# Diffusion backbone with a Conformer and an mLSTM layer: the seam before the last MLP and the last output rows rearranged

## The chip, the cores and the metric

The kernel runs on one core of one Trainium2 chip. The metric is the device time of one execution in microseconds (us), as the median of several runs; lower is better.

## The reference, cut to what matters

Two layers work on 256 latent tokens (the stream that is returned) and 256 context tokens of width 1024. What the change touches is the end of the second layer, on the latent tokens alone:

```python
h = layer_norm(ALPHA * h + g1 * y, ln1_g[i], ln1_b[i])            # y: the mLSTM's output, through w_down
h = layer_norm(ALPHA * h + g2 * sq_relu_mlp(modulate(h, sh2, sc2), mlp_w1[i], mlp_w2[i]), ln2_g[i], ln2_b[i])
# sq_relu_mlp(u) = square(relu(u @ w1)) @ w2        w1: 1024x4096, w2: 4096x1024
# sh1, sc1, g1, sh2, sc2, g2 = split(silu(c) @ ada_w[i] + ada_b[i], 6)      "adaLN", each 1024 wide
```

The gate `g2` comes from the last two of twelve blocks of 512 columns ("units" 10 and 11) of `ada_w[1]`; it is wanted only when the MLP's result is added.

## The kernel before, in words

Every matrix product is done in single precision by splitting both operands into a high and a low part (`split`: ScalarE rounds the high part, L152, VectorE subtracts for the low part, L153) and adding three products in PSUM. The weights stream in 1 MB loads through three buffers named `raw` on SyncE's queue and are split into `wh`/`wl` (or `wx`, a separate set of eight).

The rows of the stream lie in `R` (in the trace `res`): 128 partitions, two blocks t = 0, 1 of 128 tokens, 1024 columns, used as two halves (`HF`). The names below are those of the trace: `mm` (three PSUM banks), `ln`, `cv` (two each), `fl` (one) are PSUM tiles, `E`, `S`, `L` small scratch tiles of 512 columns, `mv` mean, variance and 1/sqrt of a row, `G` the gate rows.

**The seam.** `down` accumulates the mLSTM's output product in four banks `acc[t][hf]`. `residual` (L1632, L1633, L1636) multiplies a bank by the gate row, adds it to `R` and takes row statistics, all on VectorE. `row_norm` aggregates them (L1641), ScalarE takes the root (L1642), VectorE the reciprocal (L1645); `ln1_rows` scales the rows (L1651). TensorE transposes the scaled rows (`turn`, L1683, into `ln` and, for one half, `cv`), and `ln1` applies gain and modulation and writes the MLP's input `x` in high and low part: for three of the four tiles ScalarE writes the high part and a full copy in `S` (L1697) and VectorE subtracts (L1698), for the fourth VectorE does it all (L1694). Between the transposes of t = 0 and t = 1 stands one adaLN unit (`ada_unit`, L335: eight small matmuls of 32 columns each, into the bank `fl`). Unit 11 follows only after the first quarter of the MLP's first product, just before the second product; its 1 MB loads share the `raw` buffers with the weights.

**The MLP** runs in four parts c. In each, `gemm` makes eight blocks of hidden values (L190, L191; the first four of c = 0 together, in three `mm` banks and one `cv`), `e1` squares them (L200, L201, L1763), and `w2_mm` adds their product (L206 to L208) to the four banks `acc[t][hf]` (two `ln`, two `cv`), which stay open over all four parts.

**The end.** In c = 3 the last six blocks are held back (`last`), and each of the four banks is finished in turn with 18 matmuls of 512 columns. After each, `residual` runs on VectorE. When both halves of t = 0 are in, `finish(0)` normalises: ScalarE scales (L1745), GpSimd multiplies by the gain row (L1746) and adds the bias row (L1747), each half is stored. `finish(1)` does the same on VectorE (L1751, L1754); the two last stores end the kernel.

The order of instructions on each engine is set when the program is built, from the code and from a planner's times; each engine then runs its list in order and waits on semaphores. `tc.issue_after(x)` places what follows behind x, `tc.keep_in_program_order` pins an instruction, `pin` does so for the adaLN matmuls.

Of the kernel before, what the change touches and what calls it, by code (L numbers as in the profile page):

```python
# [8 lines left out]
F32 = mybir.dt.float32  # L9
# [5 lines left out]
P = 128  # L15
# [55 lines left out]
def hybrid_kernel(ctx: ExitStack, tc: tile.TileContext, xT, vecs_d, wdw_d, ada0_w, ada_w, wg_d, pw1a, pw1, pw2, w1_0, w2_0,  # L71
# [28 lines left out]
    def psum(tag="mm"):  # L100
        return pp.tile([P, 512], F32, tag=tag, name=nm(tag), bufs={"mm": 3, "ln": 2, "fl": 1, "cv": 2}[tag])
# [43 lines left out]

    def raw_load(src):
        raw = wp.tile([P, 2048], F32, tag="raw", name=nm("raw"), bufs=3)
        nc.sync.dma_start(raw[:, :src.shape[-1]], src)
        return raw

    def split(hi, lo, src):
        c = nc.scalar.copy(hi, src)  # L152
# [1485 lines left out]
    def row_norm(t, pinned=False):  # L1638

        st_, mv = nst[t]  # L1640
        nc.vector.bn_aggr(mv[:, 0:2], st_.rearrange("p h c -> p (h c)"))  # L1641
        o = nc.scalar.activation(mv[:, 2:3], mv[:, 1:2], AF.Sqrt, bias=eps)  # L1642
        if pinned:
            tc.keep_in_program_order(o)
        nc.vector.reciprocal(mv[:, 2:3], mv[:, 2:3])  # L1645
        return mv

    def ln1_rows(t, pinned=False):
        mv = row_norm(t, pinned)
        for g_ in range(2):  # L1650
            o = nc.vector.tensor_scalar(R[:, t, HF[g_]], R[:, t, HF[g_]], mv[:, 0:1], mv[:, 2:3], op0=ALU.subtract,  # L1651
                                        op1=ALU.mult)
        return o.ins
# [25 lines left out]
    def turn(t, g_, tag="ln"):  # L1679

        tr = psum(tag)
        for i in range(4):
            nc.tensor.transpose(tr[:, i * P:(i + 1) * P], R[:, t, g_ * 512 + i * P:g_ * 512 + (i + 1) * P], ident)  # L1683
        return tr

    def ln1(tr, t, g_, vector=False):

        ts = BLK[t]
        y = tmp("SL"[vector])
        for i in range(4):  # L1690
            f, sl = 4 * g_ + i, slice(i * P, (i + 1) * P)
            for o_ in (u2[f][:, ts], y[:, sl]):
                if vector:
                    nc.vector.tensor_scalar(o_, tr[:, sl], ca[:, 1, f:f + 1], cb[:, 1, f:f + 1],  # L1694
                                            op0=ALU.mult, op1=ALU.add)
                else:
                    nc.scalar.activation(o_, tr[:, sl], AF.Identity, scale=ca[:, 1, f:f + 1], bias=cb[:, 1, f:f + 1])  # L1697
            nc.vector.tensor_tensor(u2[f][:, C + t * P:C + (t + 1) * P], y[:, sl], u2[f].bitcast(F32)[:, ts],  # L1698
                                    op=ALU.subtract)
# [38 lines left out]

    def finish(t):
        mv = row_norm(t)  # L1740
        o_ = [tmp("E") for _ in range(2)]
        if t == 0:
            nc.vector.scalar_tensor_tensor(mv[:, 3:4], mv[:, 0:1], -1.0, mv[:, 2:3], op0=ALU.mult, op1=ALU.mult)
            for hf in range(2):
                nc.scalar.activation(o_[hf], R[:, t, HF[hf]], AF.Identity, scale=mv[:, 2:3], bias=mv[:, 3:4])  # L1745
                nc.gpsimd.tensor_tensor(o_[hf], o_[hf], GN[:, HF[hf]], op=ALU.mult)  # L1746
                nc.gpsimd.tensor_tensor(o_[hf], o_[hf], BN[:, HF[hf]], op=ALU.add)  # L1747
                nc.sync.dma_start(out[t * P:(t + 1) * P, HF[hf]], o_[hf])
        else:
            for hf in range(2):  # L1750
                nc.vector.scalar_tensor_tensor(o_[hf], R[:, t, HF[hf]], mv[:, 0:1], GN[:, HF[hf]],  # L1751
                                               op0=ALU.subtract, op1=ALU.mult)
            for hf in range(2):
                nc.vector.scalar_tensor_tensor(o_[hf], o_[hf], mv[:, 2:3], BN[:, HF[hf]], op0=ALU.mult, op1=ALU.add)  # L1754
                nc.sync.dma_start(out[t * P:(t + 1) * P, HF[hf]], o_[hf])

    acc = None
    for c in range(4):
        hid = {}

        def e1(m, ps):
            r_, q_ = joined(ps), tmp("E")[:, :C]
            nc.vector.scalar_tensor_tensor(q_, r_, 0.0, r_, op0=ALU.max, op1=ALU.mult)  # L1763
            t_ = HD(F32R)
            hid[m] = t_[:, :C], t_[:, C:]
            split(*hid[m], q_)

        gemm(w1_1, range(4 * c, 4 * c + 4), u2, T, e1, ko=0 if c else 3 + Z.pre4, pre=pre1 if c == 0 else None)
        if c == 0:
            ada_unit()  # L1770
            acc = [[psum("ln") for _ in range(2)], [psum("cv") for _ in range(2)]]
            for i, t_ in enumerate(G5):
                rows(t_, rows_d[i + 1:i + 2])
        elif c < 3:
            if c == 1:
                gate2()
            rescale(c - 1)

        def w2_mm(w, kt, t, hf):
            ts = BLK[t]  # L1780
            mm3t(acc[t][hf], hid[kt][0][:, ts], hid[kt][1][:, ts], w[0][hf], w[1][hf],
                 c == 0 and kt == 0, c == 3 and kt == DT - 1)

        last = []
        for k2 in range(4):
            raw = raw_load(w2_1[4 * c + k2])
            for i in range(2):
                kt = 2 * k2 + i
                if c == 3 and k2 == 1:
                    last.append((kt, split_w(raw[:, i * 1024:(i + 1) * 1024], WX)))  # L1790
                    continue
                w = split_w(raw[:, i * 1024:(i + 1) * 1024])
                w = [[w_[:, sl] for sl in HF] for w_ in w]
                if c == 3 and k2 > 1:
                    last.append((kt, w))
                else:
                    for t in range(2):
                        for hf in range(2):
                            w2_mm(w, kt, t, hf)
        if last:  # L1800
            nc.scalar.activation(con.tile([P, 1], F32, name=nm("warm")), eps, AF.Sqrt)
            for t in range(2):
                for hf in range(2):
# [83 lines left out]
```

## Time and profile before

| | before |
|---|---|
| median of 3 runs | 1698.73 us |
| lowest, highest | 1697.41, 1699.22 us |
| the profiled execution: its own time | 1699.18 us |
| the profiled execution: span of the core | 1697.5 us |
| TensorE busy in the span | 98% |
| VectorE, ScalarE, GpSimd busy | 61%, 44%, 3% |

The span runs from the first to the last event of the core in the trace; the execution's own time lies 1.7 us above it. Rows of a timeline give the start in us from the span's beginning, the duration in us, the engine (PE is TensorE's matmuls, PEld its weight loads, DVE VectorE, ACT ScalarE, POOL GpSimd, SP SyncE with its DMA queue), the code line, the operation, output and inputs, a count, and in brackets the idle time just before with what ended it. A matmul's end is modelled, and neighbours overlap: the step from one start to the next tells what it costs.

### The profile page before, as it was taken

To read this page: it belongs to the slowest core of one execution; us is meant where nothing else is said; L and a number is where in the kernel's file an instruction comes from. 1 tells how busy PE (TensorE), PEld (TensorE's weight loads), DVE (VectorE), ACT (ScalarE), POOL (GpSimd) and SP (SyncE) were. 2 spreads that over 40 slices of the span, in tenths; PEclk is the share of its full clock that TensorE was granted. 3 is DMA by queue.
4 is the path that set the end of the run, shared out by engine and by line. 5 is a ranking of instruction groups with operands and counts; after the bars stand their busy time and mean duration, and the time that the engine had idled before them with its cause. 6 is when DMAs were issued, how large, how long until landed. Compare 5 with 4: busy or idle time off the path is not lost.

```text
span 1697.5 us, 22796 instructions
## 1 busy us (share of the span) xinstructions
PE 1669.2 (98%) x8878; PEld 1363.8 (80%) x8878; DVE 1033.0 (61%) x1841; ACT 744.0 (44%) x1195; POOL 44.3 (3%) x92
## 2 busy tenths in 40 slices
PE   7999999999999999999999999999999999999997
PEld 5655898878888998876788899888877878878886
DVE  5555795666645776751243653563487786776676
ACT  3312563232324476642333533442477564645443
POOL 0000000000000000000000000000011120000001
PEclk9999999999999999999999999999999999999999
DMA  8546322434424065567765752454454556756552
GB/s 340 198 156 243 111 75 95 157 128 146 145 100 148 2 211 180 183 238 252 251 214 174 251 181 105 155 189 171 157 190 176 193 195 209 257 211 229 192 184 89
DMA packets 70828, 300.54 MB, mean 177 GB/s; under 512 B 7170, under 2 KB 22018, under 8 KB 40384
## 3 DMA queue, kind: packets, MB, share of 16 engines
q1 hardware_dynamic: 53056, 284.39, 47.6%
q10 hardware_dynamic: 17664, 14.69, 2.7%
q8 instruction: 70, 1.15, 0.3%
q14 instruction: 38, 0.31, 0.1%
HBM read 283.32 MB, written 15.73 MB: 176 GB/s over the span
## 4 chain that ended last, share of the span: by engine, by line
PE 92%; DVE 5%; ACT 1%; issue 1%; DMA 1%; POOL 0%; SPq 0%; DVEq 0%; POOLq 0%; ACTq 0%
PE mm L175 17%; PE mm L178 17%; PE mm L179 17%; PE mm L190 7%; PE mm L191 4%; PE mm L206 3%; PE mm L207 3%; PE mm L208 3%; PE cv L208 2%; PE cv L207 2%; PE cv L206 2%; PE fl L335 1%; DVE wl L153 1%; PE fl L748 1%; PE cv L830 1%
## 5 line engine op out<-in xcount | busy, mean ns | idle before, releaser
L153 DVE TENSOR_TENSOR wl<-raw,wh 128x1024 fp32r<-128x1024 f32 x346 | 424.7, 1233 | 275.8 <-ACT wh L152 271.4
L152 ACT CAST wh<-raw 128x1024 fp32r<-128x1024 f32 x346 | 360.6, 1050 | 494.5 <-PE mm L178 269.0
L178 PE MATMUL mm<-u,wh 128*128 128x512 f32 (+1 forms) x808 | 292.9, 363 | 0.1
L175 PE MATMUL mm<-u,wh 128*128 128x512 f32 (+1 forms) x680 | 245.5, 361 | 0.2 <-ACT E L770 0.2
L179 PE MATMUL mm<-u,wl 128*128 128x512 f32 (+1 forms) x680 | 242.3, 357 | 0.0
L178 PEld LDWEIGHTS mm<-u,wh 128*128 128x128 f32 x808 | 153.4, 190 | 23.5 <-issue 1.8
L175 PEld LDWEIGHTS mm<-u,wh 128*128 128x128 f32 x680 | 129.2, 190 | 28.8 <-issue 9.1
L179 PEld LDWEIGHTS mm<-u,wl 128*128 128x128 f32 x680 | 129.2, 190 | 18.4 <-issue 0.2
L175 PE MATMUL mm<-xm,wh 128*128 128x512 f32 x256 | 102.2, 399 | 0.0
L206 PE MATMUL mm<-wh,xl 128*128 128x512 f32 x256 | 101.3, 396 | 0.5 <-ACT wh L152 0.5
L207 PE MATMUL mm<-wh,xl 128*128 128x512 f32 x256 | 100.9, 394 | 0.0
L179 PE MATMUL mm<-xm,wl 128*128 128x512 f32 x256 | 99.9, 390 | 0.0
L208 PE MATMUL mm<-wl,xl 128*128 128x512 f32 x256 | 99.6, 392 | 0.0
L175 PE MATMUL mm<-hid,wh 128*128 128x512 f32 (+1 forms) x256 | 93.1, 364 | 0.0
L178 PE MATMUL mm<-hid,wh 128*128 128x512 f32 (+1 forms) x256 | 92.8, 363 | 0.0
L179 PE MATMUL mm<-hid,wl 128*128 128x512 f32 (+1 forms) x256 | 92.7, 362 | 0.0
L190 PE MATMUL mm<-x,wh 128*128 128x512 f32 x232 | 81.0, 398 | 0.8 <-DVE x L1698 0.8
L416 DVE SCALAR_TENSOR_TENSOR S<-ar,cs,S 128x512 f32<-128x512 f32 x56 | 40.8, 749 | 61.3 <-DMA ar<-ada_w 61.0
L178 PE MATMUL mm<-qq,wh 128*128 128x272 f32 x256 | 73.9, 289 | 0.0
L175 PE MATMUL mm<-qq,wh 128*128 128x272 f32 x256 | 73.5, 289 | 0.0
L179 PE MATMUL mm<-qq,wl 128*128 128x272 f32 x256 | 73.5, 288 | 0.0
L190 PE MATMUL mm<-u,wh 128*128 128x512 f32 x192 | 68.6, 399 | 0.0
(507 smaller groups left out, 3277.8 us busy)
## 6 DMA issues: line engine op xcount, KB each, us to landing
raw<-w SPq DMA_DIRECT2D x64, 1024.0 KB, 4.8
raw<-wo SPq DMA_DIRECT2D x32, 1024.0 KB, 4.9
raw<-ada_w SPq DMA_DIRECT2D x26, 1024.0 KB, 5.9
ar<-ada_w SPq DMA_DIRECT2D x80, 256.0 KB, 3.4
raw<-wv SPq DMA_DIRECT2D x16, 1024.0 KB, 5.4
raw<-wqT SPq DMA_DIRECT2D x16, 1024.0 KB, 5.6
raw<-wq SPq DMA_DIRECT2D x16, 1024.0 KB, 4.9
raw<-wk SPq DMA_DIRECT2D x16, 1024.0 KB, 5.2
```

The lines of the kernel that those rows point to most:

```text
L152: c = nc.scalar.copy(hi, src)
L153: nc.vector.tensor_tensor(lo, src, hi.bitcast(F32), op=ALU.subtract)
L175: a = nc.tensor.matmul(ps, wh, xh, start=start, stop=False)
L178: nc.tensor.matmul(ps, wh, xl, start=False, stop=False)
L179: lastmm[0] = nc.tensor.matmul(ps, wl, xh, start=False, stop=stop).ins
L190: todo = [lambda s_, e_: nc.tensor.matmul(ps, wh, r[0], start=s_, stop=e_), lambda s_, e_: nc.tensor.matmul(ps[:, :n], wl, r[0][:, :n], st ...
L191: lambda s_, e_: nc.tensor.matmul(ps[:, :n], wl, r[0][:, :n], start=s_, stop=e_)]
L206: nc.tensor.matmul(ps, xh, wh, start=start, stop=False)
L207: nc.tensor.matmul(ps, xl, wh, start=False, stop=False)
L208: nc.tensor.matmul(ps, xh, wl, start=False, stop=stop)
L335: a = nc.tensor.matmul(ps[32 * j:32 * j + 32], cs[:, kt, 14 - 2 * v:46 - 2 * v], blocks[kt], start=first and kt < 4, stop=last and kt >= 4 ...
L416: nc.vector.scalar_tensor_tensor(a, w, c, a, op0=ALU.mult, op1=ALU.add)
```

## The change

It has three parts.

At the seam the banks `fl` and one `mm` change places, so that `fl` holds `acc[0][1]` instead of `acc[1][1]`. The rows of t = 0 are scaled by ScalarE (with a small VectorE operation for the offset) instead of VectorE. The four subtractions for the low parts of the first tile (`lows`) come behind the scaling of t = 1. Both adaLN units are loaded ahead of the seam, unit 11 as eight loads of 256 KB into tiles `pw` that the mLSTM has left; its first half stands behind unit 10, its second half behind the transposes of t = 1. The place before the MLP's second product is gone.

At the end `acc[1][1]` is closed after the first two blocks and added to `R` early (`part`). The remaining six blocks of that half are computed as two quarters of 256 columns in two fresh `mm` banks, each with its own residual and statistics (`quarter`).

Of the output rows t = 0, GpSimd does the first half and the lower 256 columns of the second; the upper 256 go to VectorE (`rest`), behind the statistics of the third quarter. `finish(1)` writes to `S` tiles.

```diff
     def raw_load(src):
-        nc.sync.dma_start(raw[:, :src.shape[-1]], src)
+        loaded[0] = nc.sync.dma_start(raw[:, :src.shape[-1]], src).ins
...
-                acc.extend([[psum(), psum()], [psum(), psum("fl")]])
+                acc.extend([[psum(), psum("fl")], [psum(), psum()]])
...
     def ln1_rows(t, pinned=False):
         mv = row_norm(t, pinned)
+        if t == 0:
+            o = nc.vector.scalar_tensor_tensor(mv[:, 3:4], mv[:, 0:1], -1.0, mv[:, 2:3], op0=ALU.mult, op1=ALU.mult)
+            for g_ in range(2):
+                nc.scalar.activation(R[:, t, HF[g_]], R[:, t, HF[g_]], AF.Identity, scale=mv[:, 2:3], bias=mv[:, 3:4])
+            return o.ins
...
-    def ada_unit():
+    def ada_unit(blocks, kts=range(DT)):
         pin[0] = True
-        ada_n3.mm()
+        ada_n3.mm(blocks, kts)
         pin[0] = False
 
-    ln1(turn(0, 0), 0, 0)
+    units = [ada_load(1, 10)]
+    with tc.issue_after(loaded[0]):
+        units.append(ada_load(1, 11, PW))
+    y0 = ln1(turn(0, 0), 0, 0, low=False)
     tr1 = turn(0, 1, "cv")
 
     scaled = ln1_rows(1, True)
-    ada_unit()
+    ada_unit(units[0])
+    ada_unit(units[1], range(4))
     with tc.issue_after(scaled):
+        lows(y0, 0, 0)
         ln1(turn(1, 0), 1, 0)
         tr2 = turn(1, 1)
+        ada_unit(units[1], range(4, 8))
         ln1(tr1, 0, 1, True)
         ln1(tr2, 1, 1)
...
-                nc.gpsimd.tensor_tensor(o_[hf], o_[hf], GN[:, HF[hf]], op=ALU.mult)
-                nc.gpsimd.tensor_tensor(o_[hf], o_[hf], BN[:, HF[hf]], op=ALU.add)
-                nc.sync.dma_start(out[t * P:(t + 1) * P, HF[hf]], o_[hf])
...
+            for o, sl in ((o_[0], HF[0]), (o_[1][:, LO], slice(512, 768))):
+                nc.gpsimd.tensor_tensor(o, o, GN[:, sl], op=ALU.mult)
+                nc.gpsimd.tensor_tensor(o, o, BN[:, sl], op=ALU.add)
+            nc.sync.dma_start(out[0:P, HF[0]], o_[0])
+            return o_[1]
...
+    def part(ps, sl):
+        e_ = tmp("E")[:, :ps.shape[-1]]
+        nc.vector.tensor_tensor(e_, ps, G2[:, sl], op=ALU.mult)
+        return nc.vector.tensor_tensor(R[:, 1, sl], R[:, 1, sl], e_, op=ALU.add)
+
+    def quarter(q, ps=None):
+        sl = slice(q * C, (q + 1) * C)
+        if ps is not None:
+            part(ps, sl)
...
+        return nc.vector.bn_stats(nst[1][0][:, q, :], R[:, 1, sl]).ins
+
+    def rest(o, behind):
+        sl = slice(768, 1024)
+        with tc.issue_after(behind):
+            nc.vector.tensor_tensor(o[:, HI], o[:, HI], GN[:, sl], op=ALU.mult)
+            nc.vector.tensor_tensor(o[:, HI], o[:, HI], BN[:, sl], op=ALU.add)
+        nc.sync.dma_start(out[0:P, HF[1]], o)
...
         if c == 0:
-            ada_unit()
...
-                 c == 0 and kt == 0, c == 3 and kt == DT - 1)
+                 c == 0 and kt == 0, c == 3 and kt == (1 if t and hf else DT - 1))
...
-            for t in range(2):
-                for hf in range(2):
-                    for kt, w in last:
-                        w2_mm(w, kt, t, hf)
-                    residual(t, hf, acc[t][hf], G2)
-                finish(t)
+            for hf in range(2):
+                for kt, w in last:
+                    w2_mm(w, kt, 0, hf)
+                residual(0, hf, acc[0][hf], G2)
+                if hf == 0:
+                    part(acc[1][1], HF[1])
+            held = finish(0)
+            for kt, w in last:
+                w2_mm(w, kt, 1, 0)
+            part(acc[1][0], HF[0])
+            for q in range(2):
+                quarter(q)
+            for q, sl in HALVES:
+                ps = psum()[:, :C]
+                for i, (kt, w) in enumerate(last):
+                    mm3t(ps, hid[kt][0][:, BLK[1]], hid[kt][1][:, BLK[1]], w[0][1][:, sl], w[1][1][:, sl],
+                         i == 0, i == len(last) - 1)
+                behind = quarter(2 + q, ps)
+                if q == 0:
+                    rest(held, behind)
+            finish(1)
```

How the instructions stand. The line numbers of the changed kernel are its own: L1690 is the transpose (before L1683), L337 the adaLN matmul (L335), L1710 ScalarE's copies (L1697), L1644 the root (L1642).

TensorE at the seam, before, from the transposes of t = 0 to those of t = 1 (`raw` holds an adaLN unit):

```order
L1683 MATMUL ln_13057<-ident,res 128x128 x4
L1683 MATMUL cv_13075<-ident,res 128x128 x4
L335 MATMUL fl_13085<-raw_13086,cs 32x512 x4
L335 MATMUL fl_13085<-raw_13088,cs 32x512 x4
L1683 MATMUL ln_13098<-ident,res 128x128 x4
L1683 MATMUL ln_13116<-ident,res 128x128 x4
```

The same place now, behind the transposes of t = 0 (`raw` is unit 10, `pw` unit 11):

```order
L337 MATMUL fl_13102<-raw_13058,cs 32x512 x4
L337 MATMUL fl_13102<-raw_13060,cs 32x512 x4
L337 MATMUL fl_13102<-pw_13062,cs 32x512
L337 MATMUL fl_13102<-pw_13064,cs 32x512
L337 MATMUL fl_13102<-pw_13066,cs 32x512
L337 MATMUL fl_13102<-pw_13068,cs 32x512
L1690 MATMUL ln_13119<-ident,res 128x128 x4
L1690 MATMUL ln_13137<-ident,res 128x128 x4
L337 MATMUL fl_13102<-pw_13070,cs 32x512
L337 MATMUL fl_13102<-pw_13072,cs 32x512
L337 MATMUL fl_13102<-pw_13074,cs 32x512
L337 MATMUL fl_13102<-pw_13076,cs 32x512
```

Unit 11's eight matmuls have come from behind the first quarter of the MLP to both sides of the transposes of t = 1.

ScalarE at the same place, before: the last of the eight copies of t = 0, the root of t = 1, and what follows:

```order
L1697 ACTIVATE x_13052<-ln_13057,cb_13045,ca_13044 128x128
L1697 ACTIVATE S_13062<-ln_13057,cb_13045,ca_13044 128x128
L1642 ACTIVATE mv_13006<-mv_13006,eps 128x1
L152 CAST wx_13158<-raw_13156 128x512
L1697 ACTIVATE x_13049<-ln_13098,cb_13045,ca_13044 128x128
```

And now:

```order
L1710 ACTIVATE x_13053<-ln_13078,cb_13046,ca_13045 128x128
L1710 ACTIVATE S_13083<-ln_13078,cb_13046,ca_13045 128x128
L1644 ACTIVATE mv_13007<-mv_13007,eps 128x1
L1710 ACTIVATE x_13050<-ln_13119,cb_13046,ca_13045 128x128
L1710 ACTIVATE S_13124<-ln_13119,cb_13046,ca_13045 128x128
```

The root stands behind the same eight copies; the weight cast behind it has moved to a later place.

VectorE at the end, before, from the multiply of the third bank on:

```order
L1632 TENSOR_TENSOR E_14701<-cv_13400,row_13151 128x512
L1633 TENSOR_TENSOR res<-res,E_14701 128x512
L1636 BN_STATS st_14704<-res 128x6
L1632 TENSOR_TENSOR E_14725<-cv_13401,row_13151 128x512
L1633 TENSOR_TENSOR res<-res,E_14725 128x512
L1636 BN_STATS st_14704<-res 128x6
L1641 BN_AGGR mv_14705<-st_14704 128x2
```

And now (`E_14689` is the held second half of the output rows t = 0):

```order
L1781 TENSOR_TENSOR E_14716<-cv_13413,row_13178 128x512
L1782 TENSOR_TENSOR res<-res,E_14716 128x512
L1790 BN_STATS st_14719<-res 128x6 x2
L1781 TENSOR_TENSOR E_14742<-mm_14723,row_13178 128x256
L1782 TENSOR_TENSOR res<-res,E_14742 128x256
L1790 BN_STATS st_14719<-res 128x6
L1795 TENSOR_TENSOR E_14689<-E_14689,row_13181 128x256
L1796 TENSOR_TENSOR E_14689<-E_14689,row_13182 128x256
L1781 TENSOR_TENSOR E_14768<-mm_14749,row_13178 128x256
L1782 TENSOR_TENSOR res<-res,E_14768 128x256
L1790 BN_STATS st_14719<-res 128x6
L1643 BN_AGGR mv_14720<-st_14719 128x2
```

Behind the last bank stand three operations of 256 columns instead of three of 512, and ahead of them two that GpSimd did.

More of the change, by code (lines that the diff above doesn't have):

```diff
@@ L147, in raw_load @@
         raw = wp.tile([P, 2048], F32, tag="raw", name=nm("raw"), bufs=3)
-        nc.sync.dma_start(raw[:, :src.shape[-1]], src)
+        loaded[0] = nc.sync.dma_start(raw[:, :src.shape[-1]], src).ins
         return raw
+    loaded = [None]
     def split(hi, lo, src):
@@ L1684, in turn, with lows, ln1 @@
         return tr
-    def ln1(tr, t, g_, vector=False):
+    def lows(y, t, g_):
+        for i in range(4):
+            f = 4 * g_ + i
+            nc.vector.tensor_tensor(u2[f][:, C + t * P:C + (t + 1) * P], y[:, i * P:(i + 1) * P],
+                                    u2[f].bitcast(F32)[:, BLK[t]], op=ALU.subtract)
+    def ln1(tr, t, g_, vector=False, low=True):
         ts = BLK[t]
@@ L1740, in finish @@
         mv = row_norm(t)
-        o_ = [tmp("E") for _ in range(2)]
+        o_ = [tmp("ES"[t]) for _ in range(2)]
         if t == 0:
@@ L1745, in finish @@
                 nc.scalar.activation(o_[hf], R[:, t, HF[hf]], AF.Identity, scale=mv[:, 2:3], bias=mv[:, 3:4])
-                nc.gpsimd.tensor_tensor(o_[hf], o_[hf], GN[:, HF[hf]], op=ALU.mult)
-                nc.gpsimd.tensor_tensor(o_[hf], o_[hf], BN[:, HF[hf]], op=ALU.add)
-                nc.sync.dma_start(out[t * P:(t + 1) * P, HF[hf]], o_[hf])
-        else:
-            for hf in range(2):
[L1751 to L1755, printed above, removed]
+            for o, sl in ((o_[0], HF[0]), (o_[1][:, LO], slice(512, 768))):
[4 more added lines that the diff above has]
+        for hf in range(2):
+            nc.vector.scalar_tensor_tensor(o_[hf], R[:, t, HF[hf]], mv[:, 0:1], GN[:, HF[hf]],
+                                           op0=ALU.subtract, op1=ALU.mult)
+        for hf in range(2):
+            nc.vector.scalar_tensor_tensor(o_[hf], o_[hf], mv[:, 2:3], BN[:, HF[hf]], op0=ALU.mult, op1=ALU.add)
+            nc.sync.dma_start(out[t * P:(t + 1) * P, HF[hf]], o_[hf])
+    def part(ps, sl):
[7 more added lines that the diff above has]
+        if q == 0:
+            nst[1] = con.tile([P, 4, 6], F32, name=nm("st")), con.tile([P, 4], F32, name=nm("mv"))
+        return nc.vector.bn_stats(nst[1][0][:, q, :], R[:, 1, sl]).ins
[5 more added lines that the diff above has]
+        nc.sync.dma_start(out[0:P, HF[1]], o)
     acc = None
@@ L1801, in hybrid_kernel @@
             nc.scalar.activation(con.tile([P, 1], F32, name=nm("warm")), eps, AF.Sqrt)
-            for t in range(2):
-                for hf in range(2):
-                    for kt, w in last:
-                        w2_mm(w, kt, t, hf)
-                    residual(t, hf, acc[t][hf], G2)
-                finish(t)
+            for hf in range(2):
+                for kt, w in last:
[15 more added lines that the diff above has]
+                behind = quarter(2 + q, ps)
+                if q == 0:
+                    rest(held, behind)
+            finish(1)
     close_pool()
```

6 lines of the change are left out of this document (4 added, 2 removed).

## The prediction

> **What bounds the kernel now.** I read the page first, then the waits of the seam, then the timelines of the seam and of the end, engine by engine. The page says what the kernel lives on:
>
> ```profile
> PE 1669.2 (98%) x8878; PEld 1363.8 (80%) x8878; DVE 1033.0 (61%) x1841; ACT 744.0 (44%) x1195; POOL 44.3 (3%) x92
> ```
>
> TensorE is busy for 98% of the span, so time comes only from TensorE work taken out of its list, from its few gaps, or from the stretch behind its last matmul. The waits between 1486 and 1516 us (engine, line, whom it waited for, us in total, times, longest) hold three of those gaps; the two stretches below them (us, then busy time of PE, PEld, DVE, ACT, POOL, then clock, DMA share and GB/s) show TensorE busy for 2.22 of 4 us behind 1504 and the DMA queues empty before 1500:
>
> ```profile
> PE ln L1683 <- DVE res L1651: 1.3, 1, 1.3
> PE mm L190 <- DVE x L1698: 0.8, 1, 0.8
> PE fl L335 <- DVE E L1632: 0.5, 1, 0.5
> ...
> 1496.00:1500.00 4.00, 4.00 (x20) 3.30 (x19) 3.50 (x8) 0.29 (x1) 0.00 (x0) 1.00 0.00 0
> ...
> 1504.00:1508.00 4.00, 2.22 (x14) 1.84 (x15) 3.70 (x14) 2.92 (x9) 0.00 (x0) 1.00 0.90 334
> ```
>
> At the other end the chain that ended last (start, us, engine, tile, line) leaves TensorE with its last matmul and is VectorE's alone; the timeline row under it is the aggregation, from which on the change leaves every operation as it is:
>
> ```profile
> 1688.43 0.70 DVE E L1632
> 1689.15 1.39 DVE res L1633
> 1690.57 0.70 DVE st L1636
> ...
> 1691.29 0.21 DVE L1641 BATCH_NORM_AGGREGATE mv<-st 128x2 f32<-128x12 f32 x1
> ```
>
> From the last matmul to the aggregation pass 2.86 us (1688.43 to 1691.29). So the change can earn at three places: adaLN unit 11, the gaps of the seam, these 2.86 us.
>
> **Unit 11 leaves its old place.** TensorE's timeline there:
>
> ```profile
> 1529.37 0.39 PE L190 MATMUL mm<-x,wh 128*128 128x512 f32 x1
> 1529.69 1.92 PE L335 MATMUL fl<-raw,cs 128*32 128x512 f32 x16
> 1531.55 0.50 PE L206 MATMUL ln<-wh,hid 128*128 128x512 f32 x1
> ```
>
> From the L190 matmul to the first of the second product pass 2.18 us. With the unit gone the step is that of a 512-column matmul, and the rows of 18 of them in a bank of the end give it:
>
> ```profile
> 1680.07 0.39 PE L206 MATMUL cv<-wx,hid 128*128 128x512 f32 x1
> ...
> 1684.15 0.39 PE L206 MATMUL cv<-wx,hid 128*128 128x512 f32 x1
> ```
>
> 4.08 us for 18 is 0.23 each, so the place gives back 2.18 - 0.23 = 1.95 us, fully on the path, since nothing else ends there. It is earned only if the eight matmuls fit into the gaps of the seam; a unit costs TensorE 1.86 us there (1529.69 to 1531.55), a half 0.93.
>
> **The seam.** Its rows, by engine:
>
> ```profile
> 1501.77 1.92 PE L335 MATMUL fl<-raw,cs 128*32 128x512 f32 x16 [0.51 <-DVE E L1632]
> 1505.01 1.09 PE L1683 MATMUL ln<-ident,res 128*128 128x128 f32 x8 [1.32 <-DVE res L1651]
> 1506.86 0.50 PE L190 MATMUL mm<-x,wh 128*128 128x512 f32 x1 [0.77 <-DVE x L1698]
> ...
> 1498.07 1.00 DVE L1651 TENSOR_SCALAR res<-res,mv 128x512 f32<-128x512 f32 x2
> 1498.99 0.68 DVE L1632 TENSOR_TENSOR E<-mm,G 128x512 f32<-128x512 f32 x1
> 1504.32 1.00 DVE L1651 TENSOR_SCALAR res<-res,mv 128x512 f32<-128x512 f32 x2
> 1506.52 0.29 DVE L1698 TENSOR_TENSOR x<-S,x 128x128 fp32r<-128x128 f32 x1 [0.24 <-ACT S L1697]
> ...
> 1502.93 0.48 ACT L1697 ACTIVATE x<-ln,cb,ca 128x128 fp32r<-128x128 f32 x1
> 1503.28 0.49 ACT L1697 ACTIVATE S<-ln,cb,ca 128x128 f32<-128x128 f32 x1
> 1503.79 0.29 ACT L1642 ACTIVATE mv<-mv,eps 128x1 f32<-128x1 f32 x1
> ```
>
> *The bank.* TensorE was free at 1501.26 and stood 0.51 us for `fl`, which VectorE still had to read. With `fl` as `acc[0][1]` it is read two banks sooner, and the gap goes: the units start at 1501.26.
>
> *Rows of t = 0 on ScalarE.* The end of the kernel has the same pair of operations:
>
> ```profile
> 1683.21 0.16 DVE L1743 SCALAR_TENSOR_TENSOR mv<-mv 128x1 f32<-128x1 f32 x1
> 1683.47 1.52 ACT L1745 ACTIVATE E<-res,mv 128x512 f32<-128x512 f32 x2 [0.48 <-DVE mv L1743]
> ...
> 1500.00 0.59 PEld L1683 LDWEIGHTS ln<-ident,res 128*128 128x128 f32 x4
> ```
>
> ScalarE begins 0.26 us behind the small operation's start and needs 1.52 for both halves: 1498.07 + 0.26 + 1.52 = 1499.85, just ahead of the transposes' first weight load at 1500.00, which TensorE reaches no sooner. It costs nothing, with 0.15 us to spare for the first half and more for the second. VectorE is free some 0.7 us sooner (about 1498.25 instead of 1498.99), and its two interposed subtractions go behind the scaling. But the root of t = 1 still follows ScalarE's eight copies: the last starts at 1503.28, they step by 0.35, so the root starts at 1503.63 instead of 1503.79. All that VectorE wins shrinks to 0.16 us. The scaling then starts at 1504.16, the transposes at 1504.85, and the first complete `x`, which came at 1506.81 with its subtraction, at 1506.65; VectorE has the four postponed subtractions done by then (2 x 0.5 for the scaling, 4 x 0.2: 1505.96).
>
> *TensorE's list.* Unit 10 from 1501.26 to 1503.12, half of unit 11 to 1504.05: hidden, as the transposes wait until 1504.85. They take 1.09 to 1505.94, the second half 0.93 to 1506.87. Before, the first product began at 1506.86, so by these rows it starts as before; if the transposes' busy time holds some overlap it starts at 1506.70. I take 0.1 us of gain, with 0 and 0.16 as ends. If the cover of the second half were gone it would cost 0.93. The copy of `fl` to scratch now stands in VectorE's list behind the second low part and waits for the second half; behind it are the low parts of the third `x` and on, which TensorE wants only after eight pairs of matmuls of 512 and 256 columns, 8 x (0.23 + 0.12) = 2.8 us (the 0.12 is shown below). It costs nothing.
>
> *The loads.* Unit 11 is moved ahead of a weight load on SyncE's queue. The queue's rows, and the landing times of the quarter size:
>
> ```profile
> 1480.91 6.87 SPq L148 DMA_DIRECT2D raw<-ada_w  x2
> 1491.71 0.33 SPq L148 DMA_DIRECT2D raw<-w  x1
> ...
> ar<-ada_w SPq DMA_DIRECT2D x80, 256.0 KB, 3.4
> ```
>
> The second load of unit 10 is out by 1487.8. The eight behind it, at 0.33 us each, are out by about 1490.5 if none waits for an earlier landing; the weight load behind them waited for its buffer until 1491.71 anyway. All 2 MB have until 1503 to 1506 to land, and from 1496 to 1500 the queues carried nothing. I cost it at nothing. The later weight loads come sooner, as two loads have left their ring of buffers; the planner now casts two more of them ahead of the hidden values' copies, which delays those by two casts. The only sign of that resource in the trace is a wait of 0.2 us:
>
> ```profile
> PEld mm L190 <- DVE E L201: 0.2, 1, 0.2
> ```
>
> Each later block of hidden values is again 2.8 us of matmuls, which pass before its bank is wanted, so I take 0, with 0.3 as a loss.
>
> Seam: 1.95 + 0.1 = 2.05 us, between 1.65 and 2.1.
>
> **The end.** First TensorE: two consecutive matmuls of 256 columns step by 0.12 us,
>
> ```profile
> 589.73 0.28 PE L175 MATMUL mm<-hid,wh 128*128 128x256 f32 x1
> 589.85 0.28 PE L178 MATMUL mm<-hid,wh 128*128 128x256 f32 x1
> ```
>
> so two quarters take 36 x 0.12 = 4.32 us instead of 4.08, and TensorE ends 0.24 us later. The early `part` runs beside the first banks, in VectorE's waits. Then GpSimd against VectorE:
>
> ```profile
> 1685.07 1.18 DVE L1633 TENSOR_TENSOR res<-res,E 128x512 f32<-128x512 f32 x1
> ...
> 1684.41 1.29 POOL L1746 TENSOR_TENSOR E<-E,row 128x512 f32<-128x512 f32 x1 [284.53 <-PE cv L208]
> 1685.78 1.62 POOL L1747 TENSOR_TENSOR E<-E,row 128x512 f32<-128x512 f32 x1
> 1687.36 1.28 POOL L1746 TENSOR_TENSOR E<-E,row 128x512 f32<-128x512 f32 x1
> 1688.72 1.26 POOL L1747 TENSOR_TENSOR E<-E,row 128x512 f32<-128x512 f32 x1
> ...
> L201 DVE TENSOR_TENSOR E<-mm,E 128x256 f32<-128x256 f32 x47 | 19.8, 421 | 14.9 <-ACT E L200 14.8
> ```
>
> VectorE's add of two SBUF operands, some 0.7 us by itself, took 1.18 and 1.39 where GpSimd was at work, and both ended 0.55 us behind the end of a GpSimd operation (1685.70 to 1686.25; 1689.98 to 1690.53), while the multiply of a PSUM bank at 1688.43 kept its 0.70. The Trainium skill's page "SBUF — State Buffer", section "Who interferes with whom", says that a VectorE instruction with two SBUF inputs and a GpSimd instruction that reads SBUF lock each other out for a whole instruction, whichever starts first; these rows agree. By that rule `rest`, itself two such operations, meets GpSimd too.
>
> Now the walk. Up to the end of the third bank's add at 1686.25 nothing changes. Then two statistics of 256 columns (0.42 each, overlapping: to 1687.0), multiply (to 1687.4), and the third quarter's add, just as GpSimd starts its third operation, halved to about 0.65. If VectorE gets in first and is never held: add to 1687.9, statistics to 1688.3, `rest` to 1689.1, and the last quarter's multiply, add and statistics at 0.46 from start to start: aggregation at 1690.45, a gain of 0.85 us. If it is held both times, the add ends at 1688.3 and the first of `rest` at 1689.25; aggregation at 1691.0, a gain of 0.3. TensorE's last matmul, at 1688.63, is no bound in either. I take 0.45, nearer to the held case, as that is what both rows show.
>
> **The sum.** 2.05 + 0.45 = 2.5 us. The profiled execution would go from 1699.18 to 1696.7; its time lies 0.45 above the median, so the median goes from 1698.73 to **1696.2**, 0.15% less.
>
> **The rivals.**
>
> *Slower: unit 11 lands late.* The matmuls stand in TensorE's list ahead of the first product, so each us of lateness is a us of the kernel. If the eight loads landed one behind the other at the 3.4 us of their row, the fifth would be there at 1487.8 + 17 = 1504.8 and the eighth at 1515.0, 9.1 us behind 1505.94: 1696.2 + 9.1 = 1705.3. It loses against before once the eighth lands behind 1508.4. Against it stand the empty queues from 1496 on.
>
> *Faster: both open costs at their best.* ScalarE's copies or the root come a little sooner, so that VectorE's 0.7 us count in part and the product starts 0.4 sooner, and VectorE wins the port: 1.95 + 0.4 + 0.85 + up to 0.3 from the median's scatter = 3.5 us, 1695.2.
>
> *The end gives nothing,* because `rest` and the held add eat the shorter tail: 1698.73 - 2.05 = 1696.7.
>
> *The change does not hide the second half:* it stands behind the transposes and the `x` are ready at once: 0.93 lost, 1697.1.
>
> **How the numbers follow.** The shown runs lie from 1697.41 to 1699.22, so 0.2%, or 3.4 us, is about what a measurement of this kernel can tell from no change. The forecast has 0.44, the empty end 0.09, the open half 0.07: all within 0.2%, together 0.60. The faster case has 0.33, the late loads 0.07. The range takes in both sides of the open costs and the runs' scatter of 0.9 to a side: from 1694.5 to 1698.3; below it lies part of the faster case, above it the late loads.
>
> **What would show it.** Right: no adaLN matmuls behind 1510, three quarters of the 16 instructions of the two units ahead of the transposes with no wait for a load, the first product within 0.2 us of 1506.8, the second product some 2 us sooner; at the end an aggregation 2.3 to 2.9 us sooner than 1691.29. Wrong: a DMA wait at L337, a gap of TensorE over 0.3 us between 1518 and 1530, or VectorE waiting on TensorE in the last quarter, which would make TensorE's added 0.24 us the bound.

## The result, and the profile after

The changed kernel takes 1695.52 us (median of 20 runs, 1694.10 to 1697.91), the kernel before 1698.25 us beside it (20 runs, 1696.81 to 1700.75): ratio 0.9984, 95% interval 0.9978 to 0.9990, or 2.7 us less with 1.7 to 3.7 as its bounds. The forecast was 2.5 us less and a median of 1696.2 us; it set out from 1698.73, the median of three runs, so that 0.5 of the 0.7 us between 1696.2 and 1695.52 lie in that start.

A difference of two spans does not show where this came from. Of the profiled executions' 3.9 us (1699.18 to 1695.29, spans 1697.5 and 1693.6), part arose long before the seam. The same matmul in the timelines of before and, below it, after, 1400 us ahead of the change:

```profile
80.86 1.02 PE L800 MATMUL mm<-A,lt 128*128 128x512 f32 x2
```

```profile
79.91 1.02 PE L802 MATMUL mm<-A,lt 128*128 128x512 f32 x2
```

0.95 us of lead stands there already, and 1.31 us at the first aggregation of the seam (1497.30 before, 1495.99 after). So all comparisons below are made of three distances inside one trace: **A**, from the aggregation of t = 0 at the seam (L1641 before, L1643 after) to the first product (L190, L192); **B**, from there to the start of the third of the last four banks; **C**, from there to the last aggregation.

The landmarks of before stand in the prediction but for the first, which is this:

```profile
1497.30 0.21 DVE L1641 BATCH_NORM_AGGREGATE mv<-st 128x2 f32<-128x12 f32 x1
```

Those of after, the first product and the last aggregation again in the rows further down:

```profile
1495.99 0.21 DVE L1643 BATCH_NORM_AGGREGATE mv<-st 128x2 f32<-128x12 f32 x1
...
1676.69 0.39 PE L208 MATMUL cv<-wx,hid 128*128 128x512 f32 x1
```

| kernel | A | B | C | sum |
|---|---|---|---|---|
| before | 9.56 | 173.21 | 11.22 | 193.99 |
| after | 9.58 | 171.12 | 10.92 | 191.62 |
| the seam's part alone | 9.58 | 171.13 | 11.24 | 191.95 |
| the end's part alone | 9.57 | 173.22 | 10.92 | 193.71 |
| second unit in its old place | 9.42 | 173.20 | 10.92 | 193.54 |
| rows on VectorE again | 9.57 | 171.13 | 10.92 | 191.62 |
| bank exchanged back | 9.58 | 171.11 | 10.92 | 191.61 |
| both of these | 9.58 | 171.10 | 10.92 | 191.60 |
| whole second unit ahead of the transposes | 9.54 | 171.13 | 10.92 | 191.59 |
| whole second unit behind them | 10.44 | 170.92 | 10.91 | 192.27 |
| product of `part` in PSUM | 9.59 | 171.13 | 10.28 | 191.00 |
| root of t = 1 earlier | 8.88 | 171.12 | 10.92 | 190.92 |
| the three edits together | 8.89 | 171.11 | 9.97 | 189.97 |
| the changed kernel again | 9.59 | 171.11 | 10.93 | 191.63 |

Where nothing was altered, the distances agree to 0.03 us over all these kernels, which ran on several chips. After against before: A nothing, B 2.09, C 0.30, in sum 2.37 us.

TensorE's timeline of the seam after (L337 the adaLN units, L1690 the transposes, L192 the first product) shows the new order and the one wait that is left in it, for VectorE's rows of t = 1 (the trace has two records for each adaLN matmul, so that a unit's eight are x16 and half a unit's four x8):

```profile
1499.88 1.92 PE L337 MATMUL fl<-raw,cs 128*32 128x512 f32 x16
1501.62 1.04 PE L337 MATMUL fl<-pw,cs 128*32 128x512 f32 x8
1503.56 1.09 PE L1690 MATMUL ln<-ident,res 128*128 128x128 f32 x8 [0.90 <-DVE res L1658]
1504.57 1.07 PE L337 MATMUL fl<-pw,cs 128*32 128x512 f32 x8
1505.57 0.50 PE L192 MATMUL mm<-x,wh 128*128 128x512 f32 x1
```

The 0.51 us wait for `fl` is gone, and so is the 0.77 us wait for `x`: the first complete `x` is there at 1505.35, before TensorE is through with the second half. On ScalarE and VectorE:

```profile
1501.36 0.21 DVE L1643 BATCH_NORM_AGGREGATE mv<-st 128x2 f32<-128x12 f32 x1
1501.96 0.49 ACT L1710 ACTIVATE S<-ln,cb,ca 128x128 f32<-128x128 f32 x1
1502.30 0.33 ACT L1644 ACTIVATE mv<-mv,eps 128x1 f32<-128x1 f32 x1
1502.66 0.16 DVE L1647 RECIPROCAL mv<-mv 128x1 f32<-128x1 f32 x1 [1.09 <-ACT mv L1644]
1505.06 0.29 DVE L1712 TENSOR_TENSOR x<-S,x 128x128 fp32r<-128x128 f32 x1
```

VectorE has its statistics of t = 1 at 1501.57 and then stands 1.09 us for the root, which waits in ScalarE's list behind the eighth copy. At the end, VectorE (L1781 multiply, L1782 add, L1790 statistics, L1795 and L1796 `rest`) and GpSimd:

```profile
1681.70 1.16 DVE L1782 TENSOR_TENSOR res<-res,E 128x512 f32<-128x512 f32 x1
1682.89 0.75 DVE L1790 BATCH_NORM_STATS2 st<-res 128x6 f32<-128x256 f32 x2
1683.56 0.41 DVE L1781 TENSOR_TENSOR E<-mm,row 128x256 f32<-128x256 f32 x1
1684.01 0.99 DVE L1782 TENSOR_TENSOR res<-res,E 128x256 f32<-128x256 f32 x1
1685.03 0.43 DVE L1790 BATCH_NORM_STATS2 st<-res 128x6 f32<-128x256 f32 x1
1685.37 0.50 DVE L1795 TENSOR_TENSOR E<-E,row 128x256 f32<-128x256 f32 x1
1685.90 0.42 DVE L1796 TENSOR_TENSOR E<-E,row 128x256 f32<-128x256 f32 x1
...
1687.61 0.26 DVE L1643 BATCH_NORM_AGGREGATE mv<-st 128x2 f32<-128x24 f32 x1
```

```profile
1681.01 1.30 POOL L1768 TENSOR_TENSOR E<-E,row 128x512 f32<-128x512 f32 x1 [282.44 <-PE cv L210]
1682.39 1.63 POOL L1769 TENSOR_TENSOR E<-E,row 128x512 f32<-128x512 f32 x1
1683.97 0.74 POOL L1768 TENSOR_TENSOR E<-E,row 128x256 f32<-128x256 f32 x1
1684.79 0.79 POOL L1769 TENSOR_TENSOR E<-E,row 128x256 f32<-128x256 f32 x1
```

The third quarter's add starts 0.04 us behind a GpSimd operation and takes 0.99 us, where the last quarter's, with GpSimd through, takes 0.42.

### The profile page after: what moved, and what is told of

Its sections match the earlier page's. It is cut to its first block, busy times and chain, and to the rows that moved or that the text cites. A ratio compares the mean times of both kernels' runs of the same rounds, so it can differ in the third digit from the quotient of the medians.

```text
span 1693.6 us, 22853 instructions
## 1 busy us (share of the span) xinstructions
PE 1668.3 (99%) x8896; PEld 1364.7 (81%) x8896; DVE 1033.9 (61%) x1848; ACT 745.5 (44%) x1197; POOL 43.3 (3%) x92
## 4 chain that ended last, share of the span: by engine, by line
PE 93%; DVE 3%; ACT 2%; issue 1%; DMA 1%; POOL 0%; SPq 0%; DVEq 0%; ACTq 0%; POOLq 0%
PE mm L177 17%; PE mm L180 17%; PE mm L181 17%; PE mm L192 7%; PE mm L193 4%; PE mm L208 3%; PE mm L210 3%; PE mm L209 3%; PE cv L210 2%; PE cv L209 2%; PE cv L208 1%; PE fl L337 1%; PE fl L750 1%; PE cv L832 1%; PE ln L177 1%; PE ln L180 1%
## 5 line engine op out<-in xcount | busy, mean ns | idle before, releaser
L192 PE MATMUL mm<-x,wh 128*128 128x512 f32 x232 | 81.1, 398 | 0.0
L192 PE MATMUL mm<-u,wh 128*128 128x512 f32 x192 | 68.5, 398 | 0.0
```

The source lines that it names most:

```text
L192: todo = [lambda s_, e_: nc.tensor.matmul(ps, wh, r[0], start=s_, stop=e_), lambda s_, e_: nc.tensor.matmul(ps[:, :n], wl, r[0][:, :n], st ...
```

## The experiments

Each is the changed kernel (or the one before) with one thing altered; the distances are in the table. The first two and the last two have a ratio; the others are judged by the distances in their traces.

**Either part alone.** The seam alone is the changed kernel with the end's code of before; the end alone has the seam's code of before and the second unit at its old place:

```diff
-            held = finish(0)
-            for kt, w in last:
-                w2_mm(w, kt, 1, 0)
...
+            for t in range(2):
+                for hf in range(2):
+                    for kt, w in last:
+                        w2_mm(w, kt, t, hf)
+                    residual(t, hf, acc[t][hf], G2)
+                finish(t)
```

```diff
-    ada_unit(units[0])
-    ada_unit(units[1], range(4))
...
-        ada_unit(units[1], range(4, 8))
...
         if c == 0:
+            ada_unit()
```

> The seam's part of the change alone; the end as before. Theory (the prediction's sum): 2.05 us less than before, nearly all of it because one unit's worth of matmuls no longer stands behind the first product; ratio near 0.9988. In the trace: from the first batch's last aggregation to the first product the same as before (9.56 us) within 0.2 us, the start of the third of the last four banks about 2 us sooner against that aggregation, from there to the last aggregation 11.2 us as before. Rival (the whole gain comes from the end): ratio 0.9997 or more, the third bank less than 0.6 us sooner.

> The end's part of the change alone; the seam as before. Theory: 0.3 to 0.45 us less than before, ratio near 0.9998; from the start of the third of the last four banks to the last aggregation 10.9 us instead of 11.2. Rival (the end gives as much as the seam): ratio 0.999 or less, that stretch under 10.3 us.

The seam alone: ratio 0.9985 (0.9976 to 0.9994), sum 2.04 us less than before. The end alone: 0.9995 (0.9986 to 1.0004), which its runs cannot tell from nothing; the distance C, 0.30 us shorter, can. The two add up to 2.32 of the 2.37 us. The theory's numbers hold, the end at the lower bound of what was expected.

**The second unit in its old place.**

```diff
-    with tc.issue_after(loaded[0]):
-        units.append(ada_load(1, 11, PW))
...
-    ada_unit(units[1], range(4))
...
-        ada_unit(units[1], range(4, 8))
...
         if c == 0:
+            ada_unit(None)
```

> The changed kernel, but the second unit is loaded through `raw` and multiplied behind the first quarter of the MLP's first product again, as before; rows, banks and the end as changed. Theory (the seam's gain is this unit's place and nothing else): from the first batch's last aggregation to the first product 9.54 us, as with the unit ahead, and from the first product to the third of the last four banks 173.2 us instead of 171.12; from the first aggregation to the last 193.65 us instead of 191.62. Rival (part of the gain comes from scaling on ScalarE or from the bank): the whole is 193.2 us or less.

B is 2.08 us longer, A 0.16 shorter (0.12 shorter than expected): moving the unit is worth 1.92 us net, and what is left of the seam's gain, for rows, bank and postponed subtractions together, is 0.14 us. In this kernel the wait for `x` at the first product is back, which the second half of the unit otherwise fills:

```profile
1503.30 1.08 PE L1690 MATMUL ln<-ident,res 128*128 128x128 f32 x8 [1.75 <-DVE res L1658]
1505.16 0.50 PE L192 MATMUL mm<-x,wh 128*128 128x512 f32 x1 [0.77 <-DVE x L1712]
```

The theory was right to within 0.12 us; the rival's sum of 193.2 or less was not reached (193.54).

**Rows and bank, singly and together.** The first edit, the second, and then both:

```diff
     def ln1_rows(t, pinned=False):
         mv = row_norm(t, pinned)
-        if t == 0:
...
```

```diff
-                acc.extend([[psum(), psum("fl")], [psum(), psum()]])
+                acc.extend([[psum(), psum()], [psum(), psum("fl")]])
```

> The changed kernel, but the first batch's four row groups are scaled by VectorE again, as before. Theory: it costs nothing, since ScalarE's root for the second batch stands behind its eight copies in either version and ScalarE is through sooner when it has no rows to scale: from the first batch's last aggregation to the first product 9.6 us, within 0.3 us. Rival (the rows on ScalarE hide what the second half would cost): that stretch 0.5 us longer, 10.1 us.

> The changed kernel, but the second batch's second accumulator stands in the bank of the units' matmuls again, so that these wait for its statistics as before. Theory: the wait comes back (0.4 to 0.5 us before the first unit's second half of the queue), the transposes and all behind them go later by as much: from the first batch's last aggregation to the first product 9.6 + 0.4 to 0.5 us. Rival (TensorE would have stood waiting for VectorE's rows at the transposes in any case): the stretch stays at 9.6 us within 0.15.

> The changed kernel, with both the rows of the first batch on VectorE and the second batch's accumulator in the units' bank again, as before. Theory (either of the two edits alone takes the wait for the bank away, which is why undoing one showed nothing): the wait of 0.5 us ahead of the first unit's matmuls is back, the first half of the second unit ends 0.3 us ahead of the transposes, and these start about 0.1 us later: from the first batch's last aggregation to the first product 9.6 to 9.75 us. Rival (the pair of edits is what pays for the half unit): that stretch 10.0 us or more.

None of the three changes A by more than 0.01 us. For the bank alone the theory was wrong: with the rows on ScalarE, VectorE reads the last bank sooner, and the wait does not come back. With both edits undone it does, and nothing follows from it (TensorE's timeline of that kernel):

```profile
1501.37 1.92 PE L337 MATMUL fl<-raw,cs 128*32 128x512 f32 x16 [0.51 <-DVE E L1634]
1503.12 1.04 PE L337 MATMUL fl<-pw,cs 128*32 128x512 f32 x8
1504.47 1.09 PE L1689 MATMUL ln<-ident,res 128*128 128x128 f32 x8 [0.31 <-DVE res L1657]
```

The transposes start 7.57 us behind the aggregation of t = 0, exactly as in the changed kernel (1503.56 - 1495.99), because the root starts 6.3 us behind it in both (1502.30 - 1495.99; 1503.22 - 1496.90 with both undone): ScalarE's eight copies set it either way. The units start 0.58 us later (4.47 behind the aggregation instead of 3.89), and this comes off the wait ahead of the transposes, 0.31 instead of 0.90. Not even the expected 0.1 us was lost.

So rows and bank are not needed for the 0.14 us that the seam gained beside the unit. In the kernel before, the root of t = 1 started 6.49 us behind the aggregation, and here, with rows and bank as before, 6.32. Of what differs between the two, the postponed subtractions bear on this root. Before, three of them (L1698) stand between VectorE's operations on the last bank, and the aggregation of t = 1 ends at 1503.76, 0.03 us ahead of the root:

```profile
1502.36 0.28 DVE L1698 TENSOR_TENSOR x<-S,x 128x128 fp32r<-128x128 f32 x1
...
1503.16 0.47 DVE L1698 TENSOR_TENSOR x<-S,x 128x128 fp32r<-128x128 f32 x2
1503.56 0.20 DVE L1641 BATCH_NORM_AGGREGATE mv<-st 128x2 f32<-128x12 f32 x1
```

With both edits undone and the subtractions postponed it ends at 1503.02, and the root follows the last copy at the copies' own step of 0.35 us:

```profile
1502.81 0.21 DVE L1643 BATCH_NORM_AGGREGATE mv<-st 128x2 f32<-128x12 f32 x1
...
1502.87 0.49 ACT L1709 ACTIVATE S<-ln,cb,ca 128x128 f32<-128x128 f32 x1
1503.22 0.33 ACT L1644 ACTIVATE mv<-mv,eps 128x1 f32<-128x1 f32 x1
```

No run put the subtractions alone back in their old place, so whether the rows on ScalarE would have given the same without them stays open.

**The halves.** All eight matmuls of the second unit (sixteen records) ahead of the transposes, or all behind:

```diff
-    ada_unit(units[1], range(4))
+    ada_unit(units[1])
...
-        ada_unit(units[1], range(4, 8))
```

> The changed kernel, but the second unit's sixteen matmuls all stand ahead of the second batch's transposes instead of eight ahead and eight behind. Theory: the wait of 0.90 us ahead of the transposes (for VectorE's rows) takes the other eight in almost whole (1.0 us), so the transposes start at most 0.1 us later, and the first product is bound by ScalarE's copies again: from the first batch's last aggregation to the first product 9.4 to 9.5 us, against 9.58 with the halves. Rival (the halves are needed): that stretch 9.8 us or more.

> The changed kernel, but all sixteen matmuls of the second unit stand behind the second batch's transposes. Theory: TensorE itself is the bound between transposes and first product, so eight more matmuls cost their whole time: from the first batch's last aggregation to the first product 9.58 + 0.98 = 10.56 us, within 0.15. Rival (the product waits for ScalarE's copies and hides them): that stretch under 10.0 us.

Ahead, the unit fits whole into the wait, and the first product waits for `x` instead:

```profile
1503.02 1.90 PE L337 MATMUL fl<-pw,cs 128*32 128x512 f32 x16
1504.96 1.08 PE L1690 MATMUL ln<-ident,res 128*128 128x128 f32 x8
1506.93 0.50 PE L192 MATMUL mm<-x,wh 128*128 128x512 f32 x1 [0.89 <-DVE x L1712]
```

A is 9.54, a little above the 9.4 to 9.5 expected and 0.04 below the changed kernel, so cutting the unit in two brings nothing here. Behind, A is 10.44, 0.86 us more, where 0.98 was expected; B is 0.21 us shorter, which no theory had, so that the whole loss is 0.65. These 0.21 us come in small steps: from 2 to 10 us behind the first product, twelve matmuls take 2.07 to 2.09 us there and 2.12 to 2.13 in the changed kernel. Why was not found.

**The add at the end.** `part`'s product goes to PSUM, so that the add has one operand in SBUF:

```diff
-        e_ = tmp("E")[:, :ps.shape[-1]]
+        e_ = psum("fl")[:, :ps.shape[-1]]
```

> The changed kernel, but at the end `part`'s product goes to a PSUM bank instead of SBUF, so that VectorE's add (L1782) has one input in SBUF instead of two. Theory (VectorE's add with two inputs in SBUF is held while GpSimd works): the third quarter's add takes 0.45 us instead of 0.99, the third bank's 0.7 instead of 1.16, and the stretch from the start of the third of the last four banks to the last aggregation is 0.5 to 0.9 us shorter than 10.92 us. Rival (the adds are long for another reason, or GpSimd's products are what VectorE waits for next): stretch at 10.7 us or more.

C falls by 0.64 us. VectorE's rows for the third bank's add, the third quarter's add and `rest`, with GpSimd's last operation below them:

```profile
1681.26 0.69 DVE L1782 TENSOR_TENSOR res<-res,fl 128x512 f32<-128x512 f32 x1
...
1683.15 0.42 DVE L1782 TENSOR_TENSOR res<-res,fl 128x256 f32<-128x256 f32 x1
...
1684.39 0.84 DVE L1796 TENSOR_TENSOR E<-E,row 128x256 f32<-128x256 f32 x1
```

```profile
1684.05 0.90 POOL L1769 TENSOR_TENSOR E<-E,row 128x256 f32<-128x256 f32 x1
```

1.16 became 0.69 and 0.99 became 0.42, while GpSimd does the same four operations beside them; only the second operation of `rest`, which still reads two SBUF operands, is held. The rival is out: it is the second SBUF operand that makes the add long beside GpSimd. The Trainium skill's page "SBUF — State Buffer", section "Who interferes with whom", says that a VectorE instruction with at most one SBUF input, outside its two-port modes, does not contend with GpSimd; these rows agree.

**The root of t = 1 behind six of ScalarE's eight copies.**

```diff
         o = nc.scalar.activation(mv[:, 2:3], mv[:, 1:2], AF.Sqrt, bias=eps)
+        root[0] = o.ins
...
-    y0 = ln1(turn(0, 0), 0, 0, low=False)
+    tr0 = turn(0, 0)
+    y0 = ln1(tr0, 0, 0, low=False, tiles=range(3))
     tr1 = turn(0, 1, "cv")
 
     scaled = ln1_rows(1, True)
+    with tc.issue_after(root[0]):
+        ln1(tr0, 0, 0, low=False, y=y0, tiles=range(3, 4))
```

> The changed kernel, but the root of the second batch's variance stands on ScalarE behind six of the first batch's eight copies instead of behind all eight. Theory (this root is what the second batch waits for): rows and transposes 0.65 us sooner, the first product too, bound by TensorE's second half: from the first batch's last aggregation to the first product 8.9 to 9.0 us instead of 9.58. Rival (VectorE's rows or the units' matmuls bind next at once): gain under 0.3 us.

A falls by 0.70 us, to 8.88. Root on ScalarE and transposes on TensorE:

```profile
1500.55 0.31 ACT L1646 ACTIVATE mv<-mv,eps 128x1 f32<-128x1 f32 x1
1500.74 0.47 ACT L1713 ACTIVATE x<-ln,cb,ca 128x128 fp32r<-128x128 f32 x1
```

```profile
1501.79 1.08 PE L1693 MATMUL ln<-ident,res 128*128 128x128 f32 x8 [0.20 <-DVE res L1661]
1502.80 1.06 PE L337 MATMUL fl<-pw,cs 128*32 128x512 f32 x8
1503.80 0.50 PE L192 MATMUL mm<-x,wh 128*128 128x512 f32 x1
```

The wait ahead of the transposes shrinks from 0.90 to 0.20 us. Now TensorE has no room there for the unit's second half of 1.0 us, so that here the cut of the unit should be needed; that is read from these rows, and no run tried it.

**The three edits together.** To the last two comes GpSimd for all of t = 0's output rows (`rest` is gone). The changed kernel itself ran on the same chip.

```diff
-            for o, sl in ((o_[0], HF[0]), (o_[1][:, LO], slice(512, 768))):
+            for o, sl in zip(o_, HF):
...
-            nc.sync.dma_start(out[0:P, HF[0]], o_[0])
-            return o_[1]
+                nc.sync.dma_start(out[0:P, sl], o)
+            return
...
-                if q == 0:
-                    rest(held, behind)
```

> The changed kernel with three edits: the early root of the second batch, `part`'s product in PSUM, and GpSimd doing all of the first batch's output rows (VectorE none). Theory: 0.70 us from the root, 0.64 us from the add, 0.1 to 0.2 us from the rows that leave VectorE, then TensorE's quarters are the bound: from the first aggregation to the last 190.1 to 190.3 us instead of 191.62; 3.8 to 4.2 us less than before, ratio near 0.9976, and 0.9992 against the changed kernel. Rival (GpSimd, with more to do, holds VectorE's two-input operations of the last rows, or its last rows are late): from the first to the last aggregation 190.9 us or more.

> The changed kernel itself, unaltered, on the chip of the run above, so that the two can be compared: 2.0 to 2.7 us less than before, ratio 0.9984 to 0.9988; from the first aggregation to the last 191.62 us within 0.05.

The three together: 1694.19 us (7 runs) against 1698.73 for before, ratio 0.9974 (0.9964 to 0.9985), and 0.9991 against the changed kernel's 1695.79 (itself 0.9983 of before, 0.9974 to 0.9992). The two intervals overlap; the distances do not: 189.97 against 191.63 us, the first just under the 190.1 to 190.3 expected. (The changed kernel's ratio lies just outside its 0.9984 to 0.9988; its distances are within 0.01 us.) C is 9.97, that is 0.31 less than with the product in PSUM alone, where 0.1 to 0.2 was expected of the rows that leave VectorE. VectorE's last quarter now waits for TensorE:

```profile
1684.73 0.43 DVE L1787 TENSOR_TENSOR fl<-mm,row 128x256 f32<-128x256 f32 x1 [0.81 <-PE mm L210]
```

By this row the two quarters' 0.24 us of additional TensorE time stand on the path here, and in no other kernel. By the distances this version beats both kernels.

## Why the prediction was right, point by point

**The second unit.** The mechanism held, the term was a little small: 1.95 us taken, B fell by 2.09. The step from the last matmul ahead of the unit to the first behind it was counted less one ordinary step, but the matmul behind the unit was itself longer than ordinary. Before:

```profile
1531.55 0.50 PE L206 MATMUL ln<-wh,hid 128*128 128x512 f32 x1
1531.89 0.40 PE L207 MATMUL ln<-wh,hid 128*128 128x512 f32 x1
1532.13 0.40 PE L208 MATMUL ln<-wl,hid 128*128 128x512 f32 x1
```

It took 0.34 us to the next start, its neighbour 0.24. These 0.10 us went with the unit and make 2.05 of the 2.09; the other 0.04 were not traced. The Trainium skill's page "TensorEngine Tiling (Array Packing)", section "Key Properties", says that a change of the tiling mode drains TensorE; it gives no time. Going from matmuls of 32 columns to 128 is such a change, but no run here isolated it.

**The seam's start.** Root 0.16 us sooner foretold, 0.18 measured (6.49 before, 6.31 after, from the aggregation); transposes 0.15 sooner foretold, 0.14 measured (7.71, 7.57). TensorE's list foretold the first product "as before", 0 to 0.16 us sooner, and 0.1 was taken; 0.02 later was measured. The bound named for the value 0 was the right one, transposes and second half one behind the other: 2.02 us foretold, 2.01 measured (1.01 for the transposes and 1.00 for the half, where 1.09 and 0.93 were taken, so that two errors cancel). The earlier root was laid to the rows on ScalarE and the postponed subtractions together; with rows and bank undone it comes as early, so the subtractions suffice. The costs taken at nothing (rows on ScalarE, copy of `fl`, casts) were nothing: B held no new wait of TensorE.

**The bank** was credited with removing the 0.51 us wait. That step was incomplete: moving the rows removes it alone, and the wait lay beside a longer one, so its going moved nothing.

**The loads** were hidden, but not as worked out. SyncE's queue after:

```profile
1486.13 0.33 SPq L148 DMA_DIRECT2D raw<-ada_w  x1
1486.51 5.05 SPq L359 DMA_DIRECT2D pw<-ada_w  x8
1492.66 0.33 SPq L148 DMA_DIRECT2D raw<-w  x1
...
pw<-ada_w SPq DMA_DIRECT2D x8, 256.0 KB, 6.8
```

The eight took 5.05 us to issue, 0.63 each with the waits between them (an issue itself 0.33 to 0.65), not 0.33, and 6.8 us to land, not 3.4. The last was issued by 1491.6 and so in by about 1498.4, an estimate from these rows; the matmuls that need it run at 1504.57, and no wait for a load stands ahead of L337. The rival "unit 11 lands late" would have lost behind 1508.4, which is 1507.1 here, where the seam lies 1.31 us earlier: some 8.7 us to spare.

**The end.** 0.45 us taken, 0.30 measured. The step that was mis-sized is the choice between the two walks. The held walk gave 0.3 us, and it fits: third quarter's add at an end 8.2 us behind the third bank's start (measured 8.31), first of `rest` 9.2 (9.18), aggregation 10.93 (10.92). VectorE was held both times, by 0.57 us at the add (0.99 against 0.42) and 0.08 at `rest` (0.50 against 0.42); the value between the walks had no row of its own.

So three errors of 0.1 to 0.15 us (the unit too small, the product's start and the end too large) nearly cancelled, and that the sum came so close is luck in part: 2.5 foretold, 2.37 measured in the traces.

## What to carry to other kernels

Work moved into a wait is free only up to the next thing that ends late there, so list the waits of a seam in order before giving each a price: two of the edits here, rows and bank, can each remove a wait of 0.51 us that lay beside a longer one, and undoing both cost nothing. The longest wait pointed at one small operation, a root of one column queued behind eight copies on another engine, and moving it two places brought 0.70 us, five times what the seam had gained beside the unit. Where two changes of some microseconds are compared, measure distances between fixed landmarks inside a trace: they repeated to 0.03 us, while the whole runs scattered by 4 us.

## What the runs showed of the hardware that was not expected

At the two sizes seen, what follows GpSimd's end on VectorE goes by the operation's size: the held add ends 0.55 us behind GpSimd's operation at 512 columns (1682.31 to 1682.86), as before the change, but 0.29 us behind it at 256 (1684.71 to 1685.00), each some 0.14 less than the same add takes unheld (0.69 and 0.42). GpSimd's spans are rough, so the 0.14 may be theirs. GpSimd pays too: its bias addition took 1.63 us in the changed kernel and 1.30 us where VectorE's add read PSUM:

```profile
1681.97 1.30 POOL L1769 TENSOR_TENSOR E<-E,row 128x512 f32<-128x512 f32 x1
```
